# A diffusion backbone layer on one core: the first modulation by quarters of the features, with the first token tiles' products in between

## The chip, the cores and the metric

The kernel runs on one core of a Trainium2 chip. The time is the device time of the program in microseconds; before the change it was 1172.06 us, the median of three runs (1171.61 to 1172.12). The profile is that of one execution; its engines are PE (TensorE matmul, with its weight loads shown as PEld), DVE (VectorE), ACT (ScalarE), POOL (GpSimd) and SP (SyncE, which issues the transfers).

## The reference, cut to what matters

One layer: 1024 latent tokens and 256 context tokens, 1024 features. The part that the change touches is the start:

```python
silu_c  = silu(c);  silu_cc = silu(c_ctx)
mod_x = silu_c  @ w_ada + b_ada          # 6 sections of 1024: shift, scale, gate, ...
mod_c = silu_cc @ w_ada + b_ada
sh_m, sc_m, ... = split(mod_x, 6);  csh_m, csc_m, ... = split(mod_c, 6)
px = modulate(rms_norm(x,   g_pre_mix), sh_m,  sc_m)  @ w_in    # h * (1 + scale) + shift
pc = modulate(rms_norm(ctx, g_pre_mix), csh_m, csc_m) @ w_in
# px, pc are split into attention q, k, v, mLSTM q, k, v, output gate and 16 gate columns
```

Behind it come windowed attention and a chunkwise mLSTM, an output projection, and a SwiGLU sub-layer. All is fp32.

## The kernel before, in words

**Precision.** A product of two fp32 matrices is made from three fast matmuls: both operands are split into a high part (a cast to the fast format, on ACT) and a low part (the rest, a subtraction on DVE), and high x high, high x low and low x high are added up in PSUM (`mm3`, lines 77 to 79; `split`, lines 65 and 66). A plain fp32 matmul needs no split and takes two matmul records with four times the time.

**The modulation.** Only shift and scale (sections 0 and 1 of w_ada, 8.4 MB) are needed at the start. The loop at line 310 takes section 1 (scale) and then section 0 (shift), each in eight pieces of 128 rows by 1024 columns (line 315). For three pieces of each section the products are plain fp32 (`PLAIN`, weights `cz4`), for the other ten the piece is split (`split`, into `hh` and `hl`, which are free then) and multiplied by a four-column weight that holds the high and low parts of both conditioning vectors (`cs4`). The result rows (`pr`) are copied to SBUF (lines 355, 359), turned into columns by PE (`pcol`, line 362) and added to the biases: `scol` and `hcol` hold scale and shift for latent and context tokens, one column per 128 features.

**The token loop** (line 435) goes over ten tiles of 128 tokens, eight latent and two of context. For each: load (`prep_a`, line 192), sum of squares on ACT, root, reciprocal, scaling on POOL (line 204), transposition on PE (`prep_t`, line 220; tiles 6 to 9 come transposed from DRAM and get only the row of factors, line 214), scale by `scol` (`prep_m`, lines 235, 240, 243), shift by `hcol` (line 256), cast and low part (`prep_b`, lines 268, 269) into `hh`, `hl` or, for context, `ch`, `cl`. Then comes the product with the first slab (272 columns: gates, attention v, a quarter of the mLSTM v; `s1`, weights `w1h`, `w1l`) and, as filler for PE, half a tile's product with the second slab (384 columns, the rest of v; `s2`, weights `w2h`, `w2l`, loaded and split inside the loop at lines 459 to 461). Three tiles' second slab (`NFILL`) is done in the loop.

**What follows.** `gates` (from line 466) needs the gate columns of all ten tiles. It is a chain of small steps on DVE, ACT and PE, and the other seven tiles' second-slab products run under it. Then the 13 transposed tiles of w_in are projected (`tproj`, lines 608 to 611), whose first matmul marks the end of the start-up.

**Order.** A planner places the instructions of each engine by its own estimate. `keep_in_program_order` holds an instruction at its place among those held, and `issue_after(x)` keeps what stands in its block behind instruction x on that engine's queue; the transfers, all on SP's queue, are chained in that way. Large SBUF buffers come from 16 numbered slots (`R(k, ...)`), so a transfer into a slot waits until the slot's last reader is done.

Of the kernel before, what the change touches and what calls it, by code (L numbers as in the profile page):

```python
# [9 lines left out]
F32 = mybir.dt.float32  # L10
# [34 lines left out]
def body(tc, x, ctx, xtr, vecs, bcv, bada, gqm, gqf, wada, ws1, ws2, wt, wout, wfi, wfo,  # L45
# [56 lines left out]
    scol = c.tile([P, 2, KT], F32, name="scol")  # L102
    hcol = c.tile([P, 2, KT], F32, name="hcol")
# [42 lines left out]
    pool.memset(V[:, :, :, 128:129], 1.0)  # L146
# [21 lines left out]
    q1.tile([P, 64], F32, name="padw")  # L168
    cs4 = q1.tile([P, KT, 4], F32R, name="cs4")
    cz4 = q1.tile([P, KT, 4], F32, name="cz4")  # L170
    split(cs4[:, :, 0:2], cs4[:, :, 2:4], csil)
    pool.memset(cz4, 0.0)
    dve.tensor_copy(cz4[:, :, 0:2], csil)
# [4 lines left out]
    xts, hraw, xd = {}, {}, {}  # L178

# [5 lines left out]
    def prep_a2(i):  # L185
        tc.keep_in_program_order(act.activation(xts[i], xts[i], AF.Copy, scale=st[:, 10 + i:11 + i]))

    def prep_a(i, parts=(0, 1)):
# [4 lines left out]
        hraw[i] = R((2, 3)[i] if i < 2 else (12, 13, 8, 9, 10, 11)[i % 6], f"hraw{i}", (KT, P))  # L193
        if i >= XT:
            dma(hraw[i], xtr[i - XT])
        sq = act.activation(xt if i >= XT else hraw[i].rearrange("p a b -> p (a b)"), xt, AF.Square, accum_out=st[:, i:i + 1])
        if i > 1:
            tc.keep_in_program_order(sq)
        if 1 not in parts:
            tc.keep_in_program_order(act.activation(st[:, 10 + i:11 + i], st[:, i:i + 1], AF.Sqrt, bias=epst, scale=1.0 / D))  # L200
            return
        rms_r(st[:, 10 + i:11 + i], st[:, i:i + 1])
        if i < XT:
            pool.tensor_scalar(xt, xt, st[:, 10 + i:11 + i], 1.0, MUL, MUL)

    pts = {}
    XT = 6

    def prep_t(i, keep=False, parts=(0, 1)):
# [6 lines left out]
        for b in parts:  # L216
            pt = pa.tile([P, 4, P], F32, name="pt", tag="tp" if i else "mm", bufs=2 if i else 4)
            for k in range(4):
                kk = 4 * b + k
                t = pe.transpose(pt[:, k, :], xt[:, kk * P:(kk + 1) * P], ident)  # L220
                if keep and (not kk or i == 1):
                    tc.keep_in_program_order(t)
            pts.setdefault(i, []).append(pt)
# [3 lines left out]
    def prep_m(i):  # L227
# [9 lines left out]
        for b in range(2):  # L237
            if i == 1 and not b:
                for k in range(4):
                    tc.keep_in_program_order(act.activation(raw2[i][b][:, k], pts[i][b][:, k], AF.Copy,  # L240
                                                                    scale=scol[:, 0, 4 * b + k:4 * b + k + 1]))
                continue
            r = dve.tensor_tensor(raw2[i][b], pts[i][b], hcast(scol[:, i // NT, 4 * b:4 * b + 4]), MUL)
            if i == 1:
                tc.keep_in_program_order(r)

    def prep_b(i):
# [7 lines left out]
        for b in (1, 0) if i == 0 else range(2):  # L255
            r = (dve if i < 2 else pool).tensor_tensor(raws_[b], raws_[b], hcast(hcol[:, q, 4 * b:4 * b + 4]), ADD)
            if i < 2:
                tc.keep_in_program_order(r)
            if i == 0:
                w1_split(1, (1 - b,))  # L260
        for b in range(2):
            h_ = hs[b][:, :, tok]
            if i + b == 0:
                for k in range(4):
                    act.activation(h_[:, k], pts[i][b][:, k], AF.Identity, scale=scol[:, q, k:k + 1],
                                   bias=hcol[:, q, k:k + 1])
            else:
                tc.keep_in_program_order(act.copy(h_, raws_[b]))
            r = dve.tensor_tensor(ls[b][:, :, tok], raws_[b], h_.bitcast(F32), SUB)
            if i == 0:  # L270
                tc.keep_in_program_order(r)
        if i == 0:
            with tc.issue_after(last):
                prep_a(2, (0,))
            r2 = st[:, 12:13]
            tc.keep_in_program_order(dve.reciprocal(r2, r2))
            prep_a2(2)

    def slab_load(hi, lo, src, n, k0):
        for k in (0, 2):  # L280
            load_split(hi[:, k:k + 2], lo[:, k:k + 2], src[:, k:k + 2], R((14, 15)[k // 2], f"wr{n}_{k0}{k}", (2, n)))

    w1r = {}

    def w1_load(i):
        w1r[i] = R(i, f"wr1_{i}", (4, 272))
        return dma(w1r[i], ws1[:, i]).ins

    def w1_split(i, part=None):

        if part is None or -1 in part:
            for k in (0, 2):
                r = act.copy(w1h[i][:, k:k + 2], w1r[i][:, k:k + 2])
                if part:
                    tc.keep_in_program_order(r)
        for k in (0, 1) if part is None else part if part[0] >= 0 else ():
            sl = slice(2 * k, 2 * k + 2)
            r = dve.tensor_tensor(w1l[i][:, sl], w1r[i][:, sl], w1h[i][:, sl].bitcast(F32), SUB)  # L300
            if part:
                tc.keep_in_program_order(r)

    PLAIN = {1: (0, 2, 4), 0: (0, 2, 7)}
    last, nsp, late = None, 0, []

    wm = pa.tile([P, 4, P], F32, name="warm", tag="mm", bufs=4)
    for i in range(11):
        pe.matmul(wm[:, i % 4], ones, ones, start=True, stop=True)
    for sec in (1, 0):  # L310
        pr = [pa.tile([4, 512], F32, name=f"pr{sec}{i}", tag="mm", bufs=4) for i in range(2)]
        for kt in range(KT):
            w = R(8 + kt, f"wa{sec}_{kt}", (D,))
            with tc.issue_after(last) if last is not None else ExitStack():
                last = dma(w, wada[kt * P:(kt + 1) * P, sec * D:(sec + 1) * D]).ins
            if kt in PLAIN[sec]:
                ops = ((cz4, w),)
            else:
                wh, wl = (t[1 - nsp // 4 % 2][:, nsp % 4] for t in (hh, hl))
                nsp += 1  # L320
                split(wh, wl, w)
                ops = ((cs4, wh), (cs4, wl))
            ops = [(kt, *o) for o in ops]
            if (sec, kt) > (0, 2) and not sec:
                late += ops
                ops = ()
            if (sec, kt) == (0, KT - 1):

                ops = late = [late[k] for k in (0, 2, 1, 4, 3, 6, 5, 8, 7)]
            for n, (k, a, b) in enumerate(ops):  # L330
                if late and n < 2:
                    prep_t(1, True, (n,))
                for i in range(2):
                    r = pe.matmul(pr[i], a[:, k, :], b[:, i * 512:(i + 1) * 512], start=kt == 0 and n == 0,
                                  stop=kt == KT - 1 and n == len(ops) - 1)
                    if late:
                        tc.keep_in_program_order(r)
            if (sec, kt) == (0, 1):
                for i in range(2):
                    with tc.issue_after(last):  # L340
                        prep_a(i)
                        last = xd[i].ins
            if (sec, kt) == (0, 2):
                prep_t(0, True)
            if (sec, kt) == (0, 7):
                prep_m(0)
                prep_m(1)
                for i in range(2):
                    with tc.issue_after(last):
                        last = w1_load(i)  # L350
                w1_split(0)
                with tc.issue_after(last):
                    last = dma(bcr, bcast(bcv)).ins
        r4 = Vc.rearrange("p n h v -> p (n h v)")[0:4, 0:D]
        r = act.copy(r4[:, 0:512], pr[0])
        if sec == 0:
            tc.keep_in_program_order(r)
            w1_split(1, (-1,))
        dve.tensor_copy(r4[:, 512:D], pr[1])
        pc_ = pa.tile([P, KT, 4], F32, name="pcol", tag="gx", bufs=2)  # L360
        for kt in range(KT):
            pe.transpose(pc_[:, kt, :], r4[:, kt * P:(kt + 1) * P], ident[0:4, 0:4])
        for q in range(2):
            t = (hcol, scol)[sec][:, q]
            if sec:
# [3 lines left out]
            else:  # L369
                for b in (bcol(0), t):  # L370
                    tc.keep_in_program_order(dve.tensor_tensor(t, pc_[:, :, q if b is not t else 2 + q], b, ADD))
# [1669 lines left out]
```

## Time and profile before

| | |
|---|---|
| median of the runs | 1172.06 us (1171.61 to 1172.12) |
| profiled execution, and its span | 1171.69 us, 1169.9 us |
| PE / DVE / ACT / POOL busy | 1155.5 / 782.8 / 558.6 / 154.5 us |
| mean granted TensorE clock | 0.998 |
| first product of the projection | 33.94 us |
| last gate columns of the token loop (line 410) | 86.49 us |
| first matmul of the transposed projections (line 608) | 118.42 us |

In rows of the profile, a line like `L66 DVE TENSOR_TENSOR hl<-wa,hh 128x1024 fp32r<-128x1024 f32 x10 | 12.6, 1259 | 7.9 <-ACT hh L65 7.7` is a group: line of the kernel, engine, operation, output and inputs by name, shapes, count, busy time in us, mean of one in ns, and idle time of the engine ahead of it with what ended most of it. In the order of time a row begins with its start and its length in us. The chain of waits follows the work that ended last back from the end. For PE rows `128*4` is the weight (rows by columns). PE's ends are modelled, so the distance from start to start says more than the length of one.

### The profile page before, as it was taken

The numbers are of one execution on the slowest core, as the hardware profiler recorded it, in microseconds if no ns is written. First come the engines' busy times: TensorE is split into PE (matmuls) and PEld (weight loads), VectorE is DVE, ScalarE is ACT, GpSimd is POOL, SyncE is SP. The second block draws the span as 40 slices with busy tenths as digits, with TensorE's granted clock in tenths as the row PEclk, the third lists the DMA queues.
The fourth block names the chain that finished last, engine by engine and source line by source line (L and its number), as shares of the span: only waits on it lengthen the run. The fifth ranks groups of instructions, "written<-read, shape, count | busy, mean of one in ns | idle before, by whom it ended". The sixth has DMA issues, their size and how long they took to land.

```text
span 1169.9 us, 16222 instructions
## 1 busy us (share of the span) xinstructions
PE 1155.5 (99%) x5857; PEld 945.5 (81%) x5857; DVE 782.8 (67%) x1391; ACT 558.6 (48%) x1037; POOL 154.5 (13%) x201
## 2 busy tenths in 40 slices
PE   9899999999999999999999999999999999999997
PEld 3799888878888767888788888888888888888886
DVE  5874768873787643479777777767677755644557
ACT  6753442223777855877543333334343344434533
POOL 1430001263664630000000000000000000000000
PEclk9999999999999999999999999999999999999999
DMA  9722954657797605220334556566645467665853
GB/s 367 281 68 80 391 175 144 210 170 230 206 254 202 174 10 198 90 83 26 99 135 171 199 206 241 212 201 219 222 143 161 150 212 273 201 208 191 307 181 126
DMA packets 103272, 216.99 MB, mean 185 GB/s; under 512 B 10260, under 2 KB 39572, under 8 KB 101784
## 3 DMA queue, kind: packets, MB, share of 16 engines
q1 hardware_dynamic: 103192, 215.95, 55.5%
q8 instruction: 46, 0.75, 0.3%
q14 instruction: 34, 0.28, 0.1%
HBM read 159.29 MB, written 55.97 MB: 184 GB/s over the span
## 4 chain that ended last, share of the span: by engine, by line
PE 95%; DMA 2%; DVE 2%; issue 0%; ACT 0%; SPq 0%; DVEq 0%
PE xv L79 8%; PE xv L77 8%; PE xv L78 8%; PE pt L78 6%; PE pt L79 6%; PE pt L77 6%; PE t L609 4%; PE t L611 4%; PE t L608 4%; PE pt L1063 3%; PE pt L1045 3%; PE op L77 3%; PE op L78 3%; PE op L79 2%; PE fx L77 2%; PE fx L79 2%
## 5 line engine op out<-in xcount | busy, mean ns | idle before, releaser
L66 DVE TENSOR_TENSOR fo<-fr,fo 128x1024 fp32r<-128x1024 f32 x77 | 92.8, 1223 | 71.4 <-ACT fo L65 69.9
L65 ACT CAST fo<-fr 128x1024 fp32r<-128x1024 f32 x77 | 79.5, 1049 | 74.1 <-PE pt L79 38.2
L608 PE MATMUL t<-hh,th 128*128 128x512 f32 x208 | 82.4, 396 | 0.0
L609 PE MATMUL t<-hl,th 128*128 128x512 f32 x208 | 82.0, 394 | 0.0
L1445 ACT CAST wS<-wr 128x512 fp32r<-128x512 f32 x88 | 54.2, 622 | 55.4 <-PE pt L79 36.8
L1447 DVE TENSOR_TENSOR wS<-wr,wS 128x512 fp32r<-128x512 f32 x88 | 60.4, 689 | 19.7 <-ACT wS L1445 19.7
L79 PE MATMUL xv<-tT,wS 128*128 128x512 f32 x168 | 65.6, 391 | 0.0
L77 PE MATMUL xv<-tT,wS 128*128 128x512 f32 x168 | 65.6, 391 | 0.0
L78 PE MATMUL xv<-tT,wS 128*128 128x512 f32 x168 | 65.5, 390 | 0.0
L611 PE MATMUL t<-hh,tl 128*128 128x512 f32 x208 | 65.0, 393 | 0.0
L77 PE MATMUL op<-woh,mh 128*128 128x512 f32 x128 | 50.9, 397 | 0.0
L79 PE MATMUL op<-woh,ml 128*128 128x512 f32 x128 | 50.0, 390 | 0.0
L78 PE MATMUL op<-wol,mh 128*128 128x512 f32 x128 | 50.0, 390 | 0.0
L1193 DVE TENSOR_TENSOR wr<-wr 128x512 f32<-128x512 f32 x66 | 45.5, 690 | 1.4
L608 PEld LDWEIGHTS t<-hh,th 128*128 128x128 f32 x208 | 39.1, 188 | 8.3 <-issue 0.3
L1479 ACT ACTIVATE es<-es 128x512 f32<-128x512 f32 x22 | 13.9, 633 | 66.6 <-DVE es L1196 66.5
L609 PEld LDWEIGHTS t<-hl,th 128*128 128x128 f32 x208 | 39.1, 188 | 8.0 <-issue 1.2
L77 PE MATMUL pt<-fo 128*128 128x512 f32 x110 | 42.8, 389 | 0.0
L78 PE MATMUL pt<-fo 128*128 128x512 f32 x110 | 42.8, 389 | 0.0
L79 PE MATMUL pt<-fo 128*128 128x512 f32 x110 | 42.8, 389 | 0.0
L611 PEld LDWEIGHTS t<-hh,tl 128*128 128x128 f32 x208 | 37.2, 188 | 6.5 <-issue 0.3
L782 PE MATMUL s<-k,qh 128*128 128x256 f32 (+1 forms) x128 | 41.6, 336 | 0.5 <-DVE sm L784 0.5
(788 smaller groups left out, 3339.3 us busy)
## 6 DMA issues: line engine op xcount, KB each, us to landing
wr<-in_wfi SPq DMA_DIRECT2D x44, 512.0 KB, 5.2
wb<-in_wada SPq DMA_DIRECT2D x24, 512.0 KB, 5.8
s_d<-a SPq DMA_DIRECT2D x22, 512.0 KB, 6.7
bt<-in_wfo SPq DMA_DIRECT2D x44, 256.0 KB, 3.4
tb_d<-bt SPq DMA_DIRECT2D x11, 1024.0 KB, 3.9
fr<-s_d SPq DMA_DIRECT2D x44, 256.0 KB, 4.4
fr<-tb_d SPq DMA_DIRECT2D x44, 256.0 KB, 4.6
fr<-a_d SPq DMA_DIRECT2D x33, 256.0 KB, 4.3
```

The source lines that it names most:

```text
L65: act.copy(hi, raw)
L66: dve.tensor_tensor(lo, raw, hi.bitcast(F32), SUB)
L77: pe.matmul(ps, a[0], b[0], start=first, stop=False, **kw)
L78: pe.matmul(ps, a[0], b[1], start=False, stop=False, **kw)
L79: pe.matmul(ps, a[1], b[0], start=False, stop=last, **kw)
L608: pe.matmul(o, wh[:, kt], m[0], start=f, stop=False)
L609: pe.matmul(o, wh[:, kt], m[1], start=False, stop=False)
L611: pe.matmul(o, wl[:, kt], m[0], start=False, stop=l)
L782: pe.matmul(o, qh[:, h, :], k2[g][:, kc], start=True, stop=False)
L1193: dve.tensor_tensor(out, a, b, SUB)
L1445: act.copy(w[:, 0], raw)
L1447: dve.tensor_tensor(w[:, 1], raw, w[:, 0].bitcast(F32), SUB)
```

## The change

The first two sections of w_ada are packed anew in DRAM (`wmod`): quarter q holds the 256 shift and the 256 scale columns of features 256q to 256q+255 for all 1024 rows, in four pieces of 512 KB. The two slabs of w_in are packed by the same quarters of rows (`wsq`, 672 KB each). No piece of w_ada is split any more. For a quarter, eight plain fp32 matmuls (`pr_mm`) with 32-column weights (`cz`: the two conditioning vectors and 30 columns of zero) write four groups of 32 partitions of one bank, two row blocks into each group. The bank is copied out (`mod_row`), turned by four 128x128 transposes (`mod_t`), and the four groups' columns are added to the biases (`mod_col`, five DVE operations).

With the columns of a quarter, the quarter of the features of token tiles 0, 1 and 2 (`ET = 3`) is modulated (`h_ts`, on transposed tiles that `t_cp` copied to SBUF), split (`h_hi`, `h_lo`), and multiplied with that quarter of both slabs (`sq`, 12 matmuls), while the next quarters load. The order of all of this is written out by hand on every engine (`pin` is `keep_in_program_order`). PE gets extra matmuls of ones (`warm`: 20 at the start, 14 later; before it was 11). Tiles 3 to 9 then go through the loop as before, tile 3's second slab as its only filler; the second slab of tiles 4 to 9 runs under the gates. The second slab's weights are no longer loaded in the loop.

```diff
-    PLAIN = {1: (0, 2, 4), 0: (0, 2, 7)}
-    for sec in (1, 0):
-        pr = [pa.tile([4, 512], F32, name=f"pr{sec}{i}", tag="mm", bufs=4) for i in range(2)]
-        for kt in range(KT):
-            w = R(8 + kt, f"wa{sec}_{kt}", (D,))
...
-                split(wh, wl, w)
-                ops = ((cs4, wh), (cs4, wl))
...
+    def pr_mm(q, h):
+        if not h:
+            prs_[q] = pa.tile([P, 512], F32, name=f"pr{q}", tag="gx" if q < 3 else "tp", bufs=2)
+        for t in range(4):
+            pin(pe.matmul(prs_[q][32 * t:32 * t + 32], cz[:, 4 * h + t, :], was[q, 2 * h + t // 2][:, t % 2],
+                          start=not h, stop=h == 1))
+
+    def mod_row(q):
+        pin(act.copy(rr[:, 0:256], prs_[q][:, 0:256]))
+        pin(dve.tensor_copy(rr[:, 256:512], prs_[q][:, 256:512]))
+
+    def mod_t(q):
+        pcl[q] = pa.tile([P, 4, P], F32, name=f"pcol{q}", tag="gx" if q < 2 else "tp", bufs=2)
+        for k in range(4):
+            pin(pe.transpose(pcl[q][:, k, :], rr[:, k * P:(k + 1) * P], ident))
+
+    def mod_col(q):
+        f = slice(2 * q, 2 * q + 2)
+        pv_ = pcl.pop(q).rearrange("p (s b) (g c) -> p g s c b", s=2, c=32)
+        o = hs_[:, :, :, f]
+        t = bb[:, :, f].rearrange("p s (o k) -> p s o k", o=1).broadcast_to([P, 2, 2, 2])
+        for g in range(4):
+            pin(dve.tensor_tensor(o, pv_[:, g, :, 0:2], t, ADD))
+            t = o
...
+    def h_ts(i, q):
+        for k in (2 * q, 2 * q + 1):
+            pin(dve.tensor_scalar(hraw[i][:, k], hraw[i][:, k], scol[:, 0, k:k + 1], hcol[:, 0, k:k + 1], MUL, ADD))
...
+    def sq(i, q, mid=None):
...
+        for w, o, lo_, f, e in ((a1, A, 0, 1, 0), (a2, B, 0, 1, 0), (l1, A, 0, 0, 0), (a1, A, 1, 0, 1), (a2, B, 1, 0, 0), (l2, B, 0, 0, 1)):
+            for k in (k0, k0 + 1):
+                h_ = (hl if lo_ else hh)[b][:, k, i * P:(i + 1) * P]
+                r = pin(pe.matmul(o, h_, w[:, k], start=bool(f) and not q and k == k0, stop=bool(e) and q == 3 and k > k0))
+                n += 1
+                if mid and n == 6:
+                    mid()
...
+    ld("x0 m00 m01 m02 m03 w0 x1 m10 m11 m12 m13 w1 x2")
+    warm(20)
+    prep_c(0)
+    pr_mm(0, 0)
+    prep_t(0, True)
...
+    pr_mm(0, 1)
+    ld("m20 m21 m22 m23")
+    mod_row(0)
+    warm(2)
+    mod_t(0)
+    w_hi(0)
+    mod_col(0)
+    warm(6)
+    h_ts(0, 0)
+    h_hi(0, 0)
+    w_lo(0, 0)
+    h_lo(0, 0)
+    w_lo(0, 1)
+    ld("w2")
+    sq(0, 0)
...
+    sq(0, 2)
+    h_ts(2, 2)
+    h_hi(2, 2)
+    h_lo(2, 2)
+    prep_c(3, (0,))
+    w_hi(3)
+    prep_c(3, (1,))
+    w_lo(3, 0)
+    w_lo(3, 1)
...
+    sq(1, 2)
+    pr_mm(3, 1)
+    mod_row(3)
+    prep_c(4, (0,))
+    sq(2, 2, lambda: mod_t(3))
+    mod_col(3)
+    prep_c(4, (1,))
+    prep_t(3, True)
+    for i in range(ET):
+        h_ts(i, 3)
+        h_hi(i, 3)
+        h_lo(i, 3)
...
+    for i in range(ET):
+        sqe = sq(i, 3)
+        s1_out(i, sps[i][0])
+        act.copy(vrow(i)[:, 1:4, 0:128], sps[i][1].rearrange("p (h v) -> p h v", v=128))
+        if not i:
+            prep_b(3)
+        if i == 1:
+            prep_t(4, True)
...
+    for i in range(ET, NI):
...
+        with tc.issue_after(sqe) if i < ET + 2 else ExitStack():
             s1(i)
+            if i < ET + 2:
+                s2(ET, (i - ET,))
```

In the diff `w_hi` and `w_lo` split a quarter of both slabs, `prep_c` is the token tile's norm, and `ld` queues transfers: x for token tiles, m for pieces of w_ada (quarter, piece), w for the slabs' quarters.

More of the change, by code (lines that the diff above doesn't have):

```diff
@@ L237, in prep_m @@
         for b in range(2):
[L238 to L245, printed above, removed]
+            dve.tensor_tensor(raw2[i][b], pts[i][b], hcast(scol[:, i // NT, 4 * b:4 * b + 4]), MUL)
     def prep_b(i):
@@ L291, in w1_split @@
[L291 to L302, printed above, removed]
@@ L304, in body @@
-    PLAIN = {1: (0, 2, 4), 0: (0, 2, 7)}
[L305 to L309, printed above, removed]
-    for sec in (1, 0):
-        pr = [pa.tile([4, 512], F32, name=f"pr{sec}{i}", tag="mm", bufs=4) for i in range(2)]
-        for kt in range(KT):
-            w = R(8 + kt, f"wa{sec}_{kt}", (D,))
[L314 to L320, printed above, removed]
-                split(wh, wl, w)
-                ops = ((cs4, wh), (cs4, wl))
[L323 to L365, printed above, removed]
-                dve.scalar_tensor_tensor(t, pc_[:, :, q], 1.0, bcol(1), ADD, ADD)
-                dve.tensor_tensor(t, pc_[:, :, 2 + q], t, ADD)
-                dve.tensor_tensor(t, t, vec[:, VGPM:VGPM + 8], MUL)
-            else:
-                for b in (bcol(0), t):
-                    tc.keep_in_program_order(dve.tensor_tensor(t, pc_[:, :, q if b is not t else 2 + q], b, ADD))
@@ L372, in body, with warm @@
-    pool.memset(Vc[:, :, :, 128:129], 1.0)
-    ch += [R(i, f"ch{i}", (4, L), F32R) for i in range(2)]
-    cl += [R(2 + i, f"cl{i}", (4, L), F32R) for i in range(2)]
+            pin(act.copy(h_, raws_[b]))
+            dve.tensor_tensor(ls[b][:, :, tok], raws_[b], h_.bitcast(F32), SUB)
+    wm = pa.tile([P, 4, P], F32, name="warm", tag="mm", bufs=4)
+    def warm(n):
+        for i in range(n):
+            pin(pe.matmul(wm[:, i % 4], ones, ones, start=True, stop=True))
+    was, prs_ = {}, {}
```

268 lines of the change are left out of this document (169 added, 99 removed).

## The prediction

> **What bounds the kernel now.** I read the page first, then the busy time by stretches, then the chain of waits over the first 140 us.
>
> ```profile
> span 1169.9 us, 16222 instructions
> ...
> PE 95%; DMA 2%; DVE 2%; issue 0%; ACT 0%; SPq 0%; DVEq 0%
> ```
>
> The chain that ended last is PE nearly everywhere. The 5% that is not PE is where a change of order can win, so I looked for its place. The columns of the next view are PE, PEld, DVE, ACT and POOL busy (instructions), granted clock, DMA share, GB/s.
>
> ```profile
> 0.00:34.00 34.00, 29.41 (x119) 11.51 (x119) 19.62 (x32) 21.27 (x33) 3.19 (x13) 1.00 0.96 372
> 34.00:51.00 17.00, 15.30 (x103) 14.45 (x104) 14.13 (x31) 14.44 (x34) 7.69 (x7) 0.90 0.66 229
> 51.00:86.50 35.50, 35.33 (x253) 34.74 (x253) 29.44 (x72) 18.54 (x41) 17.18 (x16) 1.00 0.37 125
> 86.50:118.40 31.90, 31.90 (x188) 30.23 (x187) 13.69 (x63) 11.97 (x22) 1.02 (x3) 1.00 0.30 92
> 118.40:300.00 181.60, 181.17 (x994) 149.15 (x993) 128.80 (x220) 61.70 (x96) 50.88 (x76) 1.00 0.68 216
> ```
>
> ```profile
> 1.66 4.96 DMA wa<-in_wada
> ...
> 18.32 11.56 DMA wr<-in_ws
> ...
> 33.94 3.73 PE slab L391 x16
> ...
> 118.42 0.23 PE t L608
> ```
>
> Until 33.9 the DMA engines are full (share 0.96) and the chain lies on transfers: all of shift and scale must be there before one projection product can run. From 51 on PE has no idle time worth naming. So the place of the change is 0 to 118.4, where the projection of the 13 transposed tiles (line 608) starts. If that start moves by d, the end moves by d, since behind it PE idles 0.4 us in 181.6.
>
> **What is removed.** The ten splits of w_ada tiles, and the second slab's loads and splits in the token loop.
>
> ```profile
> L66 DVE TENSOR_TENSOR hl<-wa,hh 128x1024 fp32r<-128x1024 f32 x10 | 12.6, 1259 | 7.9 <-ACT hh L65 7.7
> L334 PE MATMUL pr<-wa,cz 128*4 128x512 f32 x24 | 11.3, 592 | 0.1
> L65 ACT CAST hh<-wa 128x1024 fp32r<-128x1024 f32 x10 | 10.5, 1048 | 8.0 <-DMA wa<-in_wada 7.9
> ```
>
> ACT waits 7.9 us for w_ada between its splits, so they lie under the transfers: taken away alone they are worth nothing. They make room on DVE (12.6) and ACT (10.5) for the new work, which stands in the same stretch.
>
> **When data come.** The new queue order is x0, four w_ada pieces, w0, x1, four pieces, w1, and so on; each piece is 0.52 MB, each w 0.67 MB (two slabs' quarter).
>
> ```profile
> 13.12 1.04 ACT L65 CAST hh<-wa 128x1024 fp32r<-128x1024 f32 x1 [0.25 <-DMA wa<-in_wada]
> ...
> 14.40 1.05 ACT L65 CAST hh<-wa 128x1024 fp32r<-128x1024 f32 x1 [0.23 <-DMA wa<-in_wada]
> ```
>
> Two casts that each waited for their transfer start 1.28 apart, so a piece costs 1.28 and a w 1.64. The second transfer landed at 1.66+4.96 = 6.6, the first then at 5.3. m03 lands at 5.3+4x1.28 = 10.4; the last, m33, has 19 pieces and 4 w behind the first: 5.3+24.3+6.6 = 36.2. SP issues far ahead of that: every reused buffer (m20 to m33, w2, w3) is read by my walk at least 5 us before its transfer's turn. If w3's buffer came free late, m33 and x4 behind it on SP would slip too.
>
> **The fp32 modulation.** Eight calls of four matmuls, 32 rows of output and 512 columns each, into four partition groups of one bank.
>
> ```profile
> 9.54 1.88 PE L334 MATMUL pr<-wa,cz 128*4 128x512 f32 x4
> ...
> 402.53 0.64 PE L1063 MATMUL pt<-ts__4307,av 128*64 128x512 f32 x1
> 402.54 0.64 PE L1063 MATMUL pt<-ts__4204,av 128*64 128x512 f32 x1
> ```
>
> A plain fp32 matmul of 512 columns is two records, 0.94 us. Alone, four would be 3.5 us to 3.8. But line 1063 writes two 64-row groups, and their records start 0.01 apart: both groups run in the time of one. Four groups of 32 are not in the trace. Bounds: 0.9 (all overlap) and 3.5 (none). I take 0.9, by the nearest row.
>
> The reverse side is the switch between shapes.
>
> ```profile
> 91.24 0.34 PE L79 MATMUL slab<-w2h,hl 128*128 128x384 f32 x1
> 91.51 0.45 PE L484 MATMUL pg<-cst,g 128*64 128x128 f32 x4
> ```
>
> The first 64-row matmul starts 0.27 after a full one that otherwise has its follower 0.17 behind: 0.1 a switch, at most 1.6 for 16 switches; I leave it to the range. The Trainium skill (TensorEngine Tiling (Array Packing), Key Properties) says that a change of tiling mode drains TensorE, which speaks against eight interruptions; the row agrees in sign, and with it the forecast below would be 1.6 later.
>
> **The products.** Each is 12 matmuls, one quarter of a tile for both slabs.
>
> ```profile
> 70.66 0.34 PE L77 MATMUL slab<-w2h,hh 128*128 128x384 f32 x1
> ...
> 72.76 0.38 PE L214 MATMUL pt<-vec,st 128*128 128x128 f32 x2
> ...
> 72.89 0.37 PE L77 MATMUL slab<-w1h,hh 128*128 128x272 f32 x1
> ...
> 76.02 0.34 PE L77 MATMUL slab<-w2h,hh 128*128 128x384 f32 x1
> ```
>
> Half a tile of the 384-wide slab is 2.10, a whole tile of the 272-wide 3.13; both slabs of a tile are 3.13+2x2.10 = 7.33, a quarter product 1.83. Ten tiles are 73.3 of the 84.5 us between 33.9 and 118.4. The other 11.2: transposes of tiles 2 to 5 at 1.04 (4.2), cold clock 1.6, waits 1.6 and a few tenths, say 1.8 (next row), and gates and small transposes the rest, 3.6.
>
> ```profile
> PE slab L79 <- DVE hl L269: 1.6, 2, 1.5
> ```
>
> **The chain from a quarter's last piece to its first product**, with these rows:
>
> ```profile
> 18.84 0.58 ACT L355 COPY Vc<-pr 4x512 f32<-4x512 f32 x1 [0.76 <-PE pr L334]
> ...
> 33.23 0.17 DVE L371 TENSOR_TENSOR hcol<-pcol,hcol 128x8 f32<-128x8 f32 x1
> ...
> 39.10 1.04 PE L220 MATMUL pt<-vec,xt 128*128 128x128 f32 x8
> ...
> 42.27 0.62 ACT L268 CAST hh<-hraw 128x512 fp32r<-128x512 f32 x1
> ...
> 46.55 0.96 DVE L461 TENSOR_TENSOR w2l<-wr,w2h 128x768 fp32r<-128x768 f32 x1 [0.94 <-ACT w2h L460]
> ...
> 65.14 0.21 DVE L451 TENSOR_SCALAR mF<-cst 128x128 f32<-128x128 f32 x1
> ```
>
> fp32 product 0.9, row copy halved between ACT and DVE 0.4 (half of 0.58 and a start), four transposes 0.5, five column sums 0.85, two scale-and-shift 0.35, cast of 256 columns 0.4, six handovers of 0.1: 4.0. From 10.4 the first product starts at 14.4.
>
> From there PE's written list up to the last product is: 12 products 22.0, six fp32 calls 5.4, transposes of tiles 1, 2 and 3 3.1, column transposes 1.5, four warm matmuls 0.9, together 32.9. That ends at 47.3 without a wait. Walking every engine's pinned order with these rows (a slab's low part 0.96, DVE), PE waits 0.6 for the first tile's low parts, 1.0 and 0.4 for later quarters, and 0.6 or more in the last: the DVE half of the last row copy stands behind the last slab split, which waits for ACT behind tile 3's square, and PE has transposes and half a product queued behind it. I take 3.0, bounds 0.5 and 6. m33 (36.2) is needed at about 41, so the transfers have 4 to 5 us to spare, and the second slab that is now loaded among them costs nothing. Each tenth of a microsecond more per piece would move m33 by 2.4.
>
> **The clock** is the other unknown.
>
> ```profile
> 35.00:40.00 5.00, 5.00 (x29) 4.79 (x28) 4.31 (x10) 4.33 (x8) 0.00 (x0) 0.66 0.91 358
> ...
> 35.89 0.43 PE L391 MATMUL slab<-w1l,hh 128*128 128x272 f32 x1
> 36.11 0.43 PE L391 MATMUL slab<-w1h,hh 128*128 128x272 f32 x1
> ```
>
> After the gaps before 33.9, matmuls of 272 columns come 0.22 apart instead of 0.127, some 16 of them: 1.6 us. I count one such stretch as the products begin, 1.7. Bounds: none, and all of the 32.9 at that rate.
>
> **Sum.** 14.4+32.9+3.0+1.7 = 52.0 for the first three tiles with both slabs. Then 7 tiles 51.3, and of the 11.2 what stays: without two tiles' transposes (2.1), cold clock and waits (3.4) 5.7. Tile 3's parts are ready about when PE asks: 1.0 for supply. The start of line 608 is 52.0+51.3+5.7+1.0 = 110.0, against 118.4: 8.4 earlier. The profiled execution took 1171.69 (span 1169.9 and 1.8 around it), which gives 1163.3; the median of the runs is 0.4 above it: 1163.5.
>
> **Rivals.**
> *Smooth start*: no waits, no cold clock, no supply stall: 5.7 more, 1158. For it: DVE and ACT get 12.6 and 10.5 us free. Against it: each engine's order is fixed, so one late piece stops all behind it.
>
> *Supply or gates*: the old loop had three tiles of second-slab work as filler; the new one has one.
>
> ```profile
> 71.48 2.15 DVE L235 SCALAR_TENSOR_TENSOR hraw<-hraw,scol,pt 128x128 f32<-128x128 f32 x8
> ...
> 74.40 1.73 DVE L269 TENSOR_TENSOR cl<-hraw,ch 128x512 fp32r<-128x512 f32 x2 [0.62 <-ACT ch L268]
> ...
> 86.41 0.17 DVE L408 TENSOR_TENSOR G<-slab,bcr 128x8 f32<-128x8 f32 x1 [3.22 <-PE slab L79]
> ...
> 111.79 0.22 DVE L532 COPY decb<-pd 128x64 f32<-128x64 f32 x1
> ```
>
> A late tile costs DVE 2.15+1.73+0.3 = 4.2, PE 3.13: four tiles lose 4.3. The gates took 111.8-86.4 = 25.4, under which PE now has 25.2 of second slab and 2.6 of its own: another 1 at most. The gain shrinks by 5.3 to 3: 1169.
>
> *Clock, the other side*: PE waits in short pieces throughout the load, and the granted clock falls as it did at 35.5. A cold stretch lasts 3.6 us and costs 1.7; one is in the sum. Five more of the ten stretches between 14 and 50, and the 8.4 are gone; with eight in all it is 3.5 slower, 1175. For it: that stretch followed gaps of a microsecond or less. Against it: the sparse start up to 34 was granted 1.00. The Trainium skill (TensorE: Matmul & The Clock Gate, Part 1) states the rule: an idle window of about 3.4 us halves the clock until a busy one has passed; by it gaps of a microsecond would not do it, and this case would be out.
>
> *The fp32 groups run one after the other*: 2.6 more for seven calls, 18.2: 9.8 slower, 1182. The pairs of line 1063 speak against it. With half the overlap it comes out even. The change would then not do what it says, since the products start too late to lie under the load.
>
> **Chances.** Forecast 0.46, smooth 0.18, supply 0.18, clock 0.12 (two thirds of it slower), serial groups 0.06. This measurement can tell about 0.2% (2.3 us) from none. Faster: 0.46+0.18+0.16 = 0.80; same 0.06; slower 0.08+0.06 = 0.14. The range goes from a little past the smooth start, 1156, to the clock case short of its worst, 1174; the likeliest case's own is 1160 to 1167.
>
> **What would show it.** Right: fp32 records of four groups starting together; first product near 14, m33 near 36, last quarter product near 52; line 608 near 110; PE without gaps between 60 and 105. Wrong: fp32 calls of 1.8 us or more, a granted clock under 0.9 in several of the stretches from 15 to 50, PE waiting for DVE in the token loop, or waits for w_ada past 40. It fails as a whole if the 8 us come back after 118, where I expect nothing to change but the start.

## The result, and the profile after

The changed kernel takes 1178.9 us (median of four runs, 1177.6 to 1179.7), the kernel before 1172.1 beside it: a ratio of 1.0058 with a 95% interval of 1.0045 to 1.0070. It is slower by 0.6%, where 0.7% faster was forecast. The profiled execution took 1177.58 us with a span of 1175.8, 5.9 longer than before.

The same five stretches of the busy time by windows as in the prediction, of the kernel after, and then four short ones (columns: PE, PEld, DVE, ACT, POOL busy with instructions; granted clock; DMA share; GB/s):

```profile
0.00:34.00 34.00, 30.09 (x200) 22.83 (x200) 13.33 (x40) 14.47 (x28) 4.40 (x13) 1.00 0.96 377
34.00:51.00 17.00, 15.32 (x101) 12.40 (x102) 13.70 (x36) 8.13 (x17) 4.61 (x5) 1.00 0.56 201
51.00:86.50 35.50, 31.44 (x221) 30.51 (x220) 26.14 (x79) 20.78 (x52) 14.64 (x17) 0.95 0.34 118
86.50:118.40 31.90, 31.90 (x193) 30.06 (x192) 11.15 (x49) 10.34 (x22) 1.07 (x3) 1.00 0.17 54
118.40:300.00 181.60, 177.40 (x951) 144.89 (x950) 128.43 (x225) 63.01 (x96) 43.38 (x73) 0.99 0.68 220
...
55.00:60.00 5.00, 5.00 (x38) 5.00 (x37) 1.70 (x8) 3.62 (x10) 3.15 (x3) 1.00 0.62 207
70.00:75.00 5.00, 1.98 (x14) 1.52 (x12) 5.00 (x22) 3.84 (x9) 4.83 (x5) 1.00 0.03 12
75.00:80.00 5.00, 4.41 (x23) 4.42 (x24) 4.87 (x7) 1.05 (x3) 2.05 (x5) 0.66 0.16 19
170.00:180.00 10.00, 5.89 (x26) 4.49 (x26) 6.29 (x12) 4.38 (x9) 2.38 (x1) 0.83 0.23 68
```

Up to 51 the change does its work: the clock is granted in full and PE now computes products there. Two places are new. From 51 to 86.5 PE idles 4.1 us, 3.0 of them at 70 to 75, with a low clock behind (0.66 at 75 to 80). And from 118.4 to 300, where nothing was edited, it idles 4.2 us instead of 0.4, again with a low clock (0.83 at 170 to 180). The waits of PE up to 300, of the kernel after (total, times, longest), name who it waited for:

```profile
PE slab L77 <- ACT hh L273: 3.6, 2, 2.6
PE slab L373 <- ACT hh L355: 3.4, 6, 1.2
PE pk L803 <- ACT cr L714: 1.9, 1, 1.9
PE pk L803 <- ACT mkc L722: 1.7, 1, 1.7
```

The first belongs to the token loop, the second to the load, the two on `pk` to the stage behind 118. Rows of the kernel after in the order of time (start, length) show each:

```profile
8.65 1.07 PE L304 MATMUL pr<-wm,cz 128*32 128x512 f32 x8
9.64 1.09 PE L241 MATMUL pt<-vec,xt 128*128 128x128 f32 x8
...
11.34 1.07 PE L304 MATMUL pr<-wm,cz 128*32 128x512 f32 x8
...
16.01 0.52 PE L373 MATMUL slab<-w1h,hh 128*128 128x272 f32 x2 [0.85 <-ACT hh L355]
...
53.81 1.03 PE L241 MATMUL pt<-vec,xt 128*128 128x128 f32 x8
56.13 0.51 PE L373 MATMUL slab<-w2l,hh 128*128 128x384 f32 x2
...
67.54 0.61 PE L235 MATMUL pt<-vec,st 128*128 128x128 f32 x4
...
69.02 3.96 DVE L256 SCALAR_TENSOR_TENSOR hraw<-hraw,hs,pt 128x128 f32<-128x128 f32 x15
```

The four groups of a plain fp32 call run together: eight records in 1.0 us. The first product starts at 16.0, the third tile's last one ends at 56.6. Then the row factors of two late tiles (line 235) come to PE only at 67.5, behind the filler and tile 5's transposes in PE's order, while DVE had been idle two thirds of 55 to 60; as soon as they are there DVE is handed fifteen products in a row. The chain of waits shows how PE's longest wait, 2.6 us, hangs on them (start, length, engine, output, line):

```profile
71.35 1.63 DVE hraw L256 x6
73.22 0.27 ACT av L510
73.65 1.05 ACT xt L216 x2
74.93 0.61 ACT hh L273
75.59 0.59 PE slab L77
```

Behind the products stand the gate sums of tile 5 on DVE, behind these ACT's copy of that tile's columns (`av`), then the square of a later tile that ACT's queue has next (`xt`), and only then the cast that PE needs. So the start of the transposed projections gains little. The group rows of their first matmul (line 700 after, 608 before) and of the gates' last copy give the first and the last start of each line, first after, then before:

```profile
L700 PE MATMUL t<-hh,th x208: 387/390/776, 117.2 to 296.9; 128*128 128x512 f32 x104
L623 DVE COPY decb<-pd x1: 218/218/218, 117.5 to 117.5; 128x64 f32<-128x64 f32 x1
```

```profile
L608 PE MATMUL t<-hh,th x208: 387/389/499, 118.3 to 291.9; 128*128 128x512 f32 x104
L532 DVE COPY decb<-pd x1: 221/221/221, 111.8 to 111.8; 128x64 f32<-128x64 f32 x1
```

The start is only 1.1 earlier, and the last of these matmuls 5.0 later. The gates end 5.7 later. What they feed are the mLSTM weights of line 634: eight tiles, each written to DRAM (`w_dr`, line 642) from a buffer that later holds something else. The timeline of ACT and of SP's queue in the kernel after:

```profile
147.86 2.87 SPq L750 DMA_DIRECT2D wb<-in_wada  x5
153.30 2.83 SPq L642 DMA_DIRECT2D w_dr<-w  x2
...
155.14 0.63 ACT L641 ACTIVATE w<-w 128x512 f32<-128x512 f32 x1 [0.38 <-DVE w L640]
...
162.86 1.28 ACT L722 ACT_TABLE_LOAD   x1 [3.21 <-DMA w_dr<-w]
164.16 0.42 ACT L722 ACTIVATE mkc<-ct 128x256 f32<-128x256 f32 x1
```

and the same of the kernel before:

```profile
140.72 0.33 SPq L551 DMA_DIRECT2D w_dr<-w  x1
...
150.80 0.42 ACT L630 ACTIVATE mkc<-ct 128x256 f32<-128x256 f32 x1 [4.00 <-DVE ct L629]
```

`mkc` (the context keys) lies in slot 8, and so does the last tile of weights, which takes the slots 6, 7, 8, 15, 5 in turn. Before, its store was issued at 140.7, 10 us ahead of the write of `mkc`; the stores of that kernel took 4.1 to 8.7 us from issue to landing. Now the last two stores are issued at 153.3 and 155.8, the last one as soon as ACT's exponential for its tile has ended (the row at 155.14). Five pieces of w_ada for another section (`wb`) were issued ahead of them on the same queue; whether these delay the landing is not shown. That the store comes 15 us later is more than the gates' 5.7: the last rows of `a_d`, from which the weights are made, are loaded from 139.8 on, where before they came at 127.0. ACT stands 3.2 us on the slot, everything in ACT's queue stands behind it, and PE waits 1.9 and 1.7 for what ACT has not done.

### The profile page after: what moved, and what is told of

It is laid out like the page before. It is cut to its first block, busy times and chain, and to the rows that moved or that the text cites. A ratio compares the mean times of both kernels' runs of the same rounds, so it can differ in the third digit from the quotient of the medians.

```text
span 1175.8 us, 16321 instructions
## 1 busy us (share of the span) xinstructions
PE 1153.5 (98%) x5905; PEld 950.8 (81%) x5905; DVE 774.1 (66%) x1417; ACT 551.0 (47%) x1032; POOL 147.5 (13%) x200
## 4 chain that ended last, share of the span: by engine, by line
PE 94%; DVE 3%; ACT 1%; DMA 1%; issue 0%; DVEq 0%; SPq 0%; POOL 0%; ACTq 0%; POOLq 0%
PE xv L79 8%; PE xv L77 8%; PE xv L78 8%; PE pt L79 6%; PE pt L77 6%; PE pt L78 6%; PE t L701 4%; PE t L700 4%; PE t L703 4%; PE pt L1155 3%; PE pt L1137 3%; PE op L79 2%; PE op L78 2%; PE op L77 2%; PE fx L77 2%; PE fx L79 2%
```

## The experiments

**Are the early products worth anything?** `e1_products_late` takes the nine products of the first three quarters out of the load and runs them behind it.

```diff
-    sq(0, 0)
...
-    sq(1, 0, lambda: mod_t(1))
+    mod_t(1)
...
     for i in range(ET):
+        for q in range(3):
+            sq(i, q)
         sqe = sq(i, 3)
```

> The changed kernel with the nine products of quarters 0 to 2 taken out of the loading stretch and run, tile by tile, right before those of quarter 3; nothing else differs. Theory (the products under the load are a real gain, though a smaller one than their 16.5 us, since without them PE reaches the last fp32 modulation when m33 lands, near 37, and not at 42.9): the third tile's last product ends near 63 instead of 56.5, the transposed projections start 5 to 8 us later, and the kernel takes 1182 to 1187 us. Rival (the products under the load bring nothing, because the last quarter's chain stands behind them): last product within 2 us of 56.5 and 1177 to 1180 us.

Measured: 1190.5 us (1190.2 to 1190.7), ratio 1.0154 (1.0139 to 1.0170), so 11.6 more than the change. The sign is the theory's, the size is larger than expected. A window of this run gives part of the reason:

```profile
34.00:51.00 17.00, 11.02 (x48) 8.44 (x48) 13.07 (x29) 6.23 (x15) 4.56 (x5) 0.70 0.61 229
```

Without products PE is idle a third of this stretch, and the clock falls to 0.70. In its load PE also waited 4.6 us for pieces of w_ada and 3.7 for row copies. The early products save their own time and keep the clock up. The loss of the change is not in them.

**Is it the filler in the token loop?** `e2_no_filler` moves tile 3's second slab from the loop to under the gates; `e3_tile5_early` takes norm and transposes of tile 5 ahead of the loop instead.

```diff
-            if i < ET + 2:
-                s2(ET, (i - ET,))
...
-        if i > ET:
-            s2(i)
+        s2(i)
```

```diff
+    chain(prep_l, 5)
+    prep_c(5)
...
+        if i == 2:
+            prep_t(5, True)
```

> The changed kernel with tile 3's second-slab product moved out of the token loop to its place under the gates, so that PE turns to tile 5's transposes 4 us earlier. Theory (tile preparation is late because PE's transposes and row factors stand behind that product; late gates are paid back after 170): the last gate columns come at 87 to 89 instead of 92.2, PE's waits near 172 shrink from 4.1 to under 2 us, 1172 to 1176 us. Rival (the preparation itself, on DVE and POOL, is too slow): last gate columns at 91 to 92, the product's 4 us are added as idle time, 1177 to 1181 us.

> The changed kernel with the load, the norm and the transposes of tile 5 moved ahead: norm right after tile 4's, transposes right after tile 2's last product. Theory (the token loop starves since tiles 5 and up are prepared late): the two waits of PE for the cast of tiles 6 and 7 (3.6 us) and the cold clock after them get smaller, last gate columns near 88, 1171 to 1175 us. Rival (DVE and POOL are slower than PE from tile 6 on, whatever the start): the waits move by less than 1 us, 1176 to 1179 us.

Measured: e2 1175.4 us (1173.7 to 1177.3), ratio 1.0030 (1.0021 to 1.0039); e3 1180.6 us (1180.3 to 1183.1), ratio 1.0077 (1.0055 to 1.0099). Taking the filler out gives 3.5 us back: the last gate columns come at 88.5 instead of 92.1, and the waits on `pk` are gone. The hole in the loop is not: PE waits 2.2 us for low parts and 2.2 for a row factor there, and the projections start at 117.8, 0.6 later than in the change. Pulling one tile's preparation forward missed what was expected of it: the time is above both ranges, the columns came at 92.9, and PE waited 2.6 us for low parts of the token loop and 1.2 for a cast in place of 3.6 for casts. One piece earlier only moved the wait.

**Are late gates enough to bring the waits behind 117?** `b1_before_fill4` is the kernel before with a fourth tile's second slab in the loop, which delays its gates.

```diff
-    NFILL = 3
+    NFILL = 4
...
-        if 3 <= i < 3 + 2 * NFILL:
-            s2((i - 3) // 2, ((i - 3) % 2,))
+        if 2 <= i < 2 + 2 * NFILL:
+            s2((i - 2) // 2, ((i - 2) % 2,))
```

> The kernel before, with one more tile's second-slab product in the token loop (four instead of three, the first half a tile earlier), and so one less under the gates. PE's work up to the transposed projections is the same, only the gates come later. Theory (late gates are paid back after 118, as the mLSTM weights on DVE and their stores push the convolution's end past the first state step): last gate columns 3 to 4 us later (near 90), transposed projections start within 1 us of 118.4, PE waits 1 to 4 us at the first state step near 171, 1174 to 1178 us. Rival (the 6 us lost behind 118 come from elsewhere, as another order of the planner): no wait there, 1171 to 1173 us.

Measured: 1170.7 us (1170.3 to 1171.8), ratio 0.9991 (0.9982 to 1.0000), no loss. The group rows of this run:

```profile
L532 DVE COPY decb<-pd x1: 218/218/218, 114.4 to 114.4; 128x64 f32<-128x64 f32 x1
L630 ACT ACTIVATE mkc<-ct x2: 417/418/418, 154.1 to 161.1; 128x256 f32<-128x256 f32 x2
```

The gates end 2.6 later, `mkc` is written 3.3 later, and PE waits for neither. This expectation fell: 2.6 us of lateness of the gates cost nothing here. Lateness has a price when the room behind it is used up. In the kernels with an unchanged turn of buffers the gates' end stood 3.9 us ahead of line 608 or more without a wait on `pk` (before, b1, e2; in e2 ACT still stood 1.4 us on the slot), and 0.2 ahead of it or behind it with the same 1.9 and 1.7 (after, e1, e3, and e6 below).

**Is it the shared slot?** `e4_slot` changes one tuple, so that the last tile of weights lies in slot 6.

```diff
-        wt_ = R((6, 7, 8, 15, 5)[n % 5], f"w{n}", (2, 4, P))
+        wt_ = R((8, 7, 6, 15, 5)[n % 5], f"w{n}", (2, 4, P))
```

> The changed kernel, the mLSTM weights' buffers in another turn: the last of the eight (w7) stands in slot 6, the sixth (w5) in slot 8, which the context's convolution output mkc takes next. Theory (behind 118 the time is lost because mkc waits for the store of w7, which stands in the transfer queue behind five w_ada pieces): the SiLU into mkc starts near 152 to 156 instead of 164, PE's two waits at the first state step (3.6 us) and the cold clock after them go, 1171 to 1174 us. Rival (DVE is late by the gates' 5.7 us anyway, and whatever slot the step takes it waits): the waits stay above 2.5 us, 1176 to 1179 us.

Measured: 1172.3 us (1170.3 to 1173.4), ratio 0.9999 (0.9988 to 1.0010), 6.6 less than the change. The same two rows of this run:

```profile
153.76 5.49 SPq L642 DMA_DIRECT2D w_dr<-w  x2
...
155.05 0.42 ACT L722 ACTIVATE mkc<-ct 128x256 f32<-128x256 f32 x1
```

The stores are as late as in the change, the projections start at the same 117.2, but `mkc` is written at 155.1 instead of 164.2 and the waits on `pk` are gone. That is the cause of the loss behind 117: a buffer's turn, in code that the change did not touch. `e5_no_filler_slot` puts e2's edit on top:

> Tile 3's second slab moved under the gates, as in the run without a filler, and the other turn of the buffers. Theory: that run still lost some 1.8 us at the state steps, which go now; 1171.5 to 1174 us. Rival (the slot matters only where the gates end with the fillers): no change against the run without a filler, 1175 us.

Measured: 1172.5 us (1171.3 to 1173.6), ratio 1.0001 (0.9992 to 1.0011). The two do not add up. With the slot free, gates that end at 114.5 instead of 117.6 buy nothing, and the start of the projections came 1.2 later (118.4) with the filler under the gates. e4 and e5 differ by the filler's place alone, and their times are the same within the noise.

**Where do the 4.6 us of the load go?** In the change POOL's scaling and shift of token tile 3 run between the last quarter's steps. `e6_chain` does the norm of tile 3 earlier and holds its modulation behind the last low part of tile 2.

```diff
+    prep_c(3)
...
-    prep_c(3, (0,))
...
-    prep_c(3, (1,))
...
-        h_lo(i, 3)
+        lo3 = h_lo(i, 3)
...
-            prep_b(3)
+            with tc.issue_after(lo3.ins):
+                prep_b(3)
```

> The changed kernel with two things moved out of the last quarter's chain: the norm of tile 3 goes ahead of the products of tile 2's second quarter (before it stood ahead of the last split of the slabs), and the modulation of tile 3 is held on DVE until tile 2's last low part. Theory (the last quarter is late because DVE and POOL work for tile 3 stands in its pinned order and slows DVE's operations at the same time): the last fp32 modulation's columns are ready 1 to 2 us earlier than 47.3, the third tile's last product ends near 54 instead of 56.5; what that gives at the end is 0 to 3 us: 1175 to 1178 us. Rival (PE's own list sets it): the last product ends within 0.7 us of 56.5.

Measured: 1177.0 us (1175.6 to 1177.7), ratio 1.0037 (1.0028 to 1.0047). The rows of this run:

```profile
53.27 0.51 PE L373 MATMUL slab<-w2l,hh 128*128 128x384 f32 x2
```

```profile
L700 PE MATMUL t<-hh,th x208: 387/389/775, 114.6 to 296.2; 128*128 128x512 f32 x104
```

The third tile ends 2.9 earlier, and the projections start 2.6 earlier. The end moves by 1.9 only: the gates end at 114.9, still behind the start, and the waits on `pk` stay. The edit takes work of DVE and of POOL on tile 3 out of the last quarter together, so what each of them had cost is not separated. `e7_all` has e2, the slot and the chain together.

> The three edits together: no filler in the token loop, the other turn of the buffers, tile 3 out of the last quarter's chain. Theory (they act on different losses and add up): 1168 to 1172 us, transposed projections start near 115, no wait over 1 us at the state steps. Rival (what is gained ahead of the token loop is lost in it, since it is bound by the preparation of tiles 6 to 9): 1171.5 to 1175 us, the same as the two edits without the chain.

Measured: 1170.6 us (1169.5 to 1172.7), ratio 0.9988 (0.9978 to 0.9999). The projections' first matmul starts at 116.7, 1.6 earlier than before. What still holds the loop is in this row of DVE:

```profile
71.31 2.47 DVE L66 TENSOR_TENSOR tl<-tw,th 128x1024 fp32r<-128x1024 f32 x1
```

It is the low part of the first transposed weights, not needed before 116. Its data are there, the planner takes it, and the row factor for which PE waits 2.2 us stands behind it.

**Is VectorE's queue what the loop hangs on, and does its start move the end?** `e8_split_late` has e7's edits and takes that split and two mask operations out of the loop; `b2_before_same` makes the same edits, with the slot's, to the kernel before; `e10_two_ahead` orders DVE's queue further.

```diff
-            twd[j] = load_split(wh, wl, wt[j], R(13 + j % 2, f"tw{j}", (KT, P)))
+            raw = R(13 + j % 2, f"tw{j}", (KT, P))
+            twd[j] = dma(raw, wt[j])
+        with tc.issue_after(av8[0].ins) if j < 2 else ExitStack():
+            split(wh, wl, raw)
...
-        if i == 4:
+        if i == 8:
             for m_, c_ in ((mF, up), (mB, lw)):
```

```diff
+        if i + 2 < NI:
+            with tc.issue_after(los[i].ins):
+                prep_m(i + 2)
```

The first block is e8's (`av8[0]` is the copy of the ninth tile's columns), the second what e10 adds (`los[i]` is tile i's last low part).

> The changed kernel with the edits of e7_all, and two pieces of VectorE work taken out of the token loop: the split of the first two tiles of transposed weights is issued behind the copy of the ninth tile's columns, and the two mask operations behind the ninth tile instead of the fifth. In e7_all the first of these splits lay on VectorE at 71.31 for 2.47 us; behind it stood the row factor of the last tile, for which TensorE waited 2.2, and two windows of a lower granted clock (0.89 and 0.77 over 5 us each) that cost about 1.7. Theory (the loop over the late tiles is set by what VectorE has in its queue, and the start of the transposed projections moves the end one for one): the wait and most of the cold stretch go, the projections start at 112.5 to 114 instead of 116.6, and the time is 1166 to 1168. Rival (VectorE is full from 60 to 75 whatever stands there, the wait only moves to the next low part): start 115.5 to 117, time 1169.5 to 1171. Rival (the start no longer moves the end): start near 113 and time still 1170 to 1171.

> The kernel before with the three edits that are not part of the change: the turn of the weight buffers of e4_slot, the late split and the late masks of e8_split_late. It tells whether a gain of e8_split_late belongs to the early products or to these edits alone. Theory (the kernel before loses nothing there: TensorE waited 1.6 us in its token loop and nothing for the masks in the weights): start of the transposed projections 117 to 118.3, time 1171 to 1172.5. Rival (the edits are a gain of their own): 1167 to 1169.5, and the early products would be worth no more than the rest.

> e8_split_late with one order more: the products with the row factors (or the scaled rows) of tile i+2 are issued behind tile i's last low part, so that no low part stands behind fifteen of them. In e7_all TensorE waited 2.2 us in two pieces for low parts that stood behind such products. Theory (the order within VectorE's queue is what is left): these waits go, start 110.5 to 112.5, time 1163.5 to 1166. Rival (VectorE's sum over the late tiles, about 4.2 us a tile against 3.13 of TensorE, is the limit, and an order cannot help): within 1 us of e8_split_late, with the wait put down to another line.

Measured: e8 1168.3 us (1166.3 to 1171.0), ratio 0.9971 (0.9961 to 0.9981); b2 1171.7 (1171.2 to 1173.1), 0.9998 (0.9989 to 1.0007); e10 1169.1 (1168.0 to 1170.0), 0.9975 (0.9966 to 0.9984). The group row of e8:

```profile
L704 PE MATMUL t<-hh,th x208: 387/389/501, 113.7 to 288.0; 128*128 128x512 f32 x104
```

The start is 4.6 earlier than before and the time 3.4 shorter, so the theory's start came out and the time just missed its 1166 to 1168. The edits alone are worth nothing to the kernel before. e10 brought nothing over e8: its start was 2.1 later (115.8), and the wait moved on to the context tiles' low parts (0.9 us for `cl`). The order of the products with row factors is not what is left.

**Where does the filler belong?** `e11_filler_in_waits` is e8 with tile 3's second slab behind the column products of tiles 5 and 6, in place of under the gates.

```diff
             s1(i)
+        if i in (5, 6):
+            s2(ET, (i - 5,))
...
-        s2(i)
+        if i > ET:
+            s2(i)
```

> e8_split_late with the second-slab product of token tile 3 (24 products of 0.17 us, 4.2 in all) taken from under the gate arithmetic and put behind the column products of tiles 5 and 6, where e8_split_late still waits 1.7 us for low parts on VectorE. Theory (work of TensorE placed inside a wait is free, and what it leaves under the gates comes off): the low-part waits go, the last gate columns come at 86 to 87.5 instead of 84.4, and the transposed projections start at 111.5 to 113 instead of 113.5; time 1166.5 to 1168.5. Rival (the products stand as one block and are not as long as the waits, so the columns come later by nearly all 4.2 us and the gates' end sets the weights' end again): start 113 to 114.5, time 1168.5 to 1170.5.

Measured: 1164.5 us (1163.4 to 1165.3), ratio 0.9930 (0.9918 to 0.9942): better than either theory allowed. Of this run, a window and the group row:

```profile
51.00:86.50 35.50, 34.72 (x254) 34.22 (x253) 27.03 (x79) 21.26 (x52) 18.63 (x20) 1.00 0.33 118
```

```profile
L707 PE MATMUL t<-hh,th x208: 387/389/497, 109.2 to 283.9; 128*128 128x512 f32 x104
```

PE now idles 0.8 us in the token loop, the last columns come at 85.4, only 1.0 later than in e8, and the projections start at 109.2, 9.1 earlier than before. The same 4.2 us of filler stood at tiles 3 and 4 in the change, ahead of the hole at 73 to 75.6; under the gates, in e8, it filled no wait in the loop; here it stands where DVE has fallen behind. e8 and e11 differ by this alone, 3.8 us in time. No run has the filler at tiles 3 and 4 together with the other edits of e11. Of the 9.1, the profiled span keeps 6.8 (1163.1 against 1169.9). Against the change e11 has five edits: the chain, the slot, the late split, the late masks, the filler's place. Against b2, the kernel before with the three of them that fit it, it is 7.2 us shorter. Between the last of these matmuls (8.0 earlier) and the end 1.2 are lost again; what takes them was not followed up.

## Why the prediction was wrong

**Right.** The fp32 call: 1.0 us where 0.9 was forecast, with all four groups in the time of one. The transfers: PE waited for none in the load, so the second slab loaded there held it up nowhere. The clock: granted in full up to 51, where I counted one cold stretch. The Trainium skill (TensorE: Matmul & The Clock Gate, Part 1) had put gaps of a microsecond out of account; in the load the trace agrees, with gaps of up to 1.2 us and a clock of 1.00.

**First product at 14.4.** It came at 16.0. The second fp32 call started at 11.3, not at 10.4, since tile 0's transposes and three warm matmuls (six records) stand ahead of it in PE's written order. From there the chain took 4.7 in place of 4.0.

**PE's list of 32.9 and waits of 3.0.** From 16.0 to 56.6 PE was busy 36.5 and idle 4.1. The list was short by 3.6, of which 1.0 is only moved work: the transposes of tile 4 (the row at 53.81) are done ahead of the last product. A product is 1.9 to 2.0 instead of 1.83, a fp32 call 1.0 instead of 0.9; these make up some 1.7 of the rest. So the third tile ended at 56.6 and not at 52.0: 1.6 late at the start, 3.6 of list, 1.1 of waits, less 1.7 for the clock. 2.9 of it came back in e6, which took the work on tile 3 out of the last quarter.

**Supply 1.0.** This is the first step that failed by its mechanism. The rival of supply named the place and had DVE's sum (4.2 a tile against PE's 3.13), but priced it as a steady rate. What the trace shows is order: DVE was idle at 55 to 60 and full from 70 on, because its input stood late in PE's order, behind the filler and tile 5's transposes; the wait was 3.6 us, and the clock behind it fell to 0.66 for 5 us, 1.7 more. Less the 1.0 of supply and the 1.0 of transposes that were done already, that makes 3.3; the stretch from 56.6 to 117.2 was 60.6 instead of 58.0, so my other terms there were some 0.7 too large. The filler alone is not the cause: without it (e2) PE still waited 4.4 us in the loop. e8 and e11 show that it is the order of the whole: with the same work for every engine, 109.2 against 117.2 (of these 8.0, 2.6 belong to the load, by e6). My start of 110.0 was reachable, but not with this order.

**"If that start moves by d, the end moves by d."** This is the step by which the sign was wrong. The start moved 1.1 earlier and the span grew by 5.9. I read the 0.4 us of idle time in 118.4 to 300 as proof that nothing there depends on anything but the start. It only said that everything else came in time. How far ahead it came was not in that number. The store of the last weights was issued 10 us ahead of the write that needs its slot, with 4.1 to 8.7 of them for landing, and it hangs on the gates' end and on the loads in SP's queue. By the terms of my own rival the gates would end 2.4 ahead of the start (25.4 against 25.2 and 2.6 of PE's work), where they had ended 6.5 ahead; measured, they ended 0.3 behind it. I priced the gates only as work under which PE might run dry. Freed of the slot the step holds in part: from before to e11 the start moves by 9.1 and the end by 6.8.

**"It fails as a whole if the 8 us come back after 118."** They did so in part. Of the 8.4 expected, 7.3 were lost ahead of 117, and another 7.0 behind it. The second loss is shown by e4. That the first lies in the load and in the loop's order is shown by e6, e8 and e11 together; how it divides between POOL's interference, the filler's place and the split of the weights is not shown, since each edit moves the planner's other choices too.

## What to carry to other kernels

An idle time of zero behind the place of a change says that what is consumed there came in time, not by how much. Before moving a start, take each late consumer, go back to the transfer or the buffer that frees it, and write down its slack: which queue it stands in, and who takes over its slot. And filler for PE has a place, not only an amount: put where the engine that feeds PE has fallen behind, it gained 3.8 us over its place under the gates (e8, e11). That it does harm when it stands ahead of the small instructions that feed that engine is a reading of the trace; with the slot free, that place and the one under the gates took the same time (e4, e5).

## What the runs showed of the hardware

**VectorE is held up while GpSimd works on SBUF.** The last quarter of the load in the kernel after, DVE and POOL in the order of time:

```profile
42.93 1.12 POOL L214 TENSOR_SCALAR xt<-xt,st 128x1024 f32<-128x1024 f32 x1 [14.51 <-DVE st L213]
43.21 1.41 DVE L341 TENSOR_TENSOR w1l<-V,w1h 128x544 fp32r<-128x544 f32 x1 [0.37 <-ACT w1h L337]
...
47.67 1.21 POOL L214 TENSOR_SCALAR xt<-xt,st 128x1024 f32<-128x1024 f32 x1 [1.96 <-DVE st L213]
47.90 1.28 DVE L259 TENSOR_TENSOR hraw<-pt,hs 128x512 f32<-128x512 f32 x2
48.85 2.21 POOL L270 TENSOR_TENSOR hraw<-hraw,hs 128x512 f32<-128x512 f32 x2
49.09 1.07 DVE L358 TENSOR_TENSOR hl<-hraw,hh 128x256 fp32r<-128x256 f32 x1
50.09 1.31 DVE L352 TENSOR_SCALAR hraw<-hraw,hs 128x128 f32<-128x128 f32 x2
```

The same low part of a slab takes 0.72 where POOL is idle, that of 256 columns 0.43, the pair of scale-and-shifts 0.60. The first ends 0.6 after POOL does, nearly as if it began only then; the product with `pt`, one of whose inputs is in PSUM, keeps its 0.64 each under POOL's work. The Trainium skill (SBUF — State Buffer, SBUF: two separate sides) describes it: the two engines share a pair of ports that one instruction holds to its end, and VectorE needs it for two inputs from SBUF or in a two-port mode. The trace agrees, with some 0.7 us lost for each of these three groups. In e6, where POOL's scaling stands elsewhere, the same low part took 0.72 (at 41.72), and a pair of scale-and-shifts that now met POOL's work took 1.40 (at 37.89). The rows of my chain were taken with POOL idle or nearly so.

**A wait of 2.2 us can halve the clock, or not.** The wait for the last tile's row factor in `e2_no_filler`, and the clock of the windows around it:

```profile
75.84 0.49 PE L235 MATMUL pt<-vec,st 128*128 128x128 f32 x2 [2.17 <-DVE st L220]
```

```profile
75.00:80.00 5.00, 3.88 (x27) 3.48 (x28) 5.00 (x16) 1.47 (x4) 1.77 (x2) 1.00 0.55 165
```

and the same wait in `e7_all`:

```profile
73.91 0.80 PE L235 MATMUL pt<-vec,st 128*128 128x128 f32 x2 [2.17 <-DVE st L220]
```

```profile
70.00:75.00 5.00, 2.83 (x18) 2.53 (x18) 5.00 (x12) 1.76 (x8) 2.42 (x5) 0.89 0.09 8
75.00:80.00 5.00, 5.00 (x34) 5.00 (x33) 4.49 (x13) 1.57 (x6) 2.49 (x2) 0.77 0.62 205
```

The wait is 2.17 us in both. In the one the clock stays at 1.00, in the other it falls to 0.89 and 0.77 in the mean of 5 us; in windows of one microsecond it is 0.50 from 74 to 77 and 1.00 again from 78 on. The Trainium skill's idle window of about 3.4 us (TensorE: Matmul & The Clock Gate, Part 1) is longer than either wait; here the measurement decides, and a hole of 2 us in the token loop has to be counted with up to 1.7 us behind it (0.11 and 0.23 of 5 us each).
